# Seven block products instead of eight in 28 projection tiles of a hybrid encoder step

## The chip, the core and the metric

The kernel runs on one core of a Trainium2 chip. The metric is the device time of one execution in microseconds, first instruction to last and what lies around it. The core has five engines that run unsynchronised: TensorE (PE; its weight loads are listed as PEld), VectorE (DVE), ScalarE (ACT), GpSimd (POOL) and SyncE (SP), whose queue issues most DMAs.

## What is computed

One layer for 1088 tokens (1024 of a new stream, 64 of a running one), all in float32:

```
y = x @ w_in                      # (1088 x 1024) @ (1024 x 8720), split by columns into
                                  # qa, ka, va, za | q/k/v of B, a, b, z_B | g_A, g_B
A: rotary on 16 of 64 dims of qa, ka; attention over the own 64-token chunk and 2 before it,
   with a sink per head;          Y_A = (attn * silu(za)) @ w_o_attn
B: causal conv + SiLU, l2norm, gated delta rule in chunks of 64, gated RMSNorm;
                                  Y_B = (rmsnorm(o) * silu(z_B)) @ w_o_delta
x' = LayerNorm(alpha * x + (sig(g_A) * Y_A + sig(g_B) * Y_B) @ w_out)
```

It also returns the last keys and values, the conv tail and the delta states.

## The kernel before

The model dimension lies on the partitions. `w_in` is cut into tiles of 128 output channels. A float32 product is made of three matmuls of a reduced-precision type: each operand is split into a high part (a copy on ACT, L85) and a low part (a subtraction on DVE, L86), and `mm3` adds hi*hi, hi*lo and lo*hi in one PSUM bank. `ring` holds the split x: eight tiles of 128 rows by 1088 tokens, hi and lo.

A projection tile (`project`) runs over three token groups of 384, 384 and 320 columns, each 8 k-tiles by 3 matmuls: 72 matmuls. Each group has a bank of the pool `pj` (three banks; the pool `bg` has five), and `evac` takes it out. `weights` loads a tile of 512 KB and splits it, one tile ahead.

Stages, in order: load and split x; two key tiles (`branch_a_keys`); `vab`, which gives values and the a, b columns with x as the stationary and 272 weight columns as the moving operand; 8 query tiles and 8 z_A tiles, in the first of which `gates` is woven (the decay of branch B, two small matmuls on its results); attention, woven with 13 merge-gate tiles; four head pairs of branch B, woven with their projections, the last 3 gate tiles (`GATES`), z_B and the output product of A; the output product of B; `w_out` and LayerNorm.

`weave(chain, fill)` writes TensorE's order by hand: each step of the chain says how many columns of fill follow it (`UNIT` = 8797 for attention). TensorE's instructions stay in that order. On the other engines and in the DMA queue a scheduler orders by priority; what is under `urgent` goes first. A tile of a pool with `bufs=n` waits until one of n buffers is free. All queues are in order at run time.

An attention unit (36 of them: 9 chunk pairs, 2 key groups, 2 halves) is `scores`, `flip` (6 transposes) and `values`. Before, iteration i runs values of unit i-2, flip of i-1, scores of i. Keys and the z_A gates stay in SBUF, queries come by DMA.

## Time and profile before

| | us |
|---|---|
| median of 3 runs | 1417.84 (1416.69 to 1418.1) |
| the profiled execution | 1418.09 |
| its span, first to last instruction | 1416.3 |
| TensorE busy | 1395.6 |
| DVE, ACT, POOL busy | 914.9, 566.3, 124.9 |
| mean granted TensorE clock | 0.998 |

The profiled execution takes 1.8 us more than its span. Matmuls overlap in the array, so the duration of one is longer than its distance to the next; where TensorE is busy without a break, the pace is the length of the stretch over the number of matmuls.

### The profile page before, as it was taken

To read this page: it belongs to the slowest core of one execution; us is meant where nothing else is said; L and a number is where in the kernel's file an instruction comes from. 1 tells how busy PE (TensorE), PEld (TensorE's weight loads), DVE (VectorE), ACT (ScalarE), POOL (GpSimd) and SP (SyncE) were. 2 spreads that over 40 slices of the span, in tenths; PEclk is the share of its full clock that TensorE was granted. 3 is DMA by queue.
4 is the path that set the end of the run, shared out by engine and by line. 5 is a ranking of instruction groups with operands and counts; after the bars stand their busy time and mean duration, and the time that the engine had idled before them with its cause. 6 is when DMAs were issued, how large, how long until landed. Compare 5 with 4: busy or idle time off the path is not lost.

```text
span 1416.3 us, 29219 instructions
## 1 busy us (share of the span) xinstructions
PE 1395.6 (99%) x11514; PEld 1303.3 (92%) x11514; DVE 914.9 (65%) x2290; ACT 566.3 (40%) x1576; POOL 124.9 (9%) x301
## 2 busy tenths in 40 slices
PE   8999999999999999999999999999999999999997
PEld 8999999899999999988999889988999889999886
DVE  5477522566555457967796777867788554555676
ACT  5333321344444344356633665256534442322000
POOL 0000000000000013121221113021221100000000
PEclk9999999999999999999999999999999999999999
DMA  8123572233432410210321103210435326564221
GB/s 275 44 108 147 204 187 66 89 102 99 144 95 90 142 50 31 72 36 16 89 83 58 31 26 104 81 52 18 156 122 182 97 76 205 170 218 144 95 90 75
DMA packets 81176, 147.52 MB, mean 104 GB/s; under 512 B 10896, under 2 KB 60304, under 8 KB 79760
## 3 DMA queue, kind: packets, MB, share of 16 engines
q1 hardware_dynamic: 67552, 135.17, 29.3%
q10 hardware_dynamic: 13488, 10.49, 2.4%
q8 instruction: 91, 1.49, 0.4%
q14 instruction: 45, 0.37, 0.1%
HBM read 101.39 MB, written 44.24 MB: 103 GB/s over the span
## 4 chain that ended last, share of the span: by engine, by line
PE 89%; DVE 6%; ACT 3%; issue 1%; DMA 1%; SPq 0%; POOL 0%; DVEq 0%; ACTq 0%
PE pj L103 66%; PE bg L103 19%; PE bg L106 4%; DVE acc L586 2%; PE pj L106 1%; ACT whi L85 1%; DVE t2k L689 0%; DVE wlo L86 0%; ACT acc L584 0%; DVE plb L593 0%; DVE t2k L691 0%; DVE ring L86 0%; DMA pl<-xT 0%; DMA plb<-prodB 0%; ACT qs L776 0%
## 5 line engine op out<-in xcount | busy, mean ns | idle before, releaser
L103 PE MATMUL pj<-ring,whi 128*128 128x384 f32 (+1 forms) x3696 | 930.5, 331 | 0.0
L103 PEld LDWEIGHTS pj<-ring,whi 128*128 128x128 f32 x3696 | 648.8, 188 | 9.9 <-issue 8.6
L103 PE MATMUL pj<-ring,wlo 128*128 128x384 f32 (+1 forms) x1848 | 611.1, 331 | 0.0
L103 PEld LDWEIGHTS pj<-ring,wlo 128*128 128x128 f32 x1848 | 347.5, 188 | 5.0 <-issue 4.6
L86 DVE TENSOR_TENSOR wlo<-wraw,whi 128x1024 fp32r<-128x1024 f32 (+2 forms) x86 | 100.9, 1173 | 78.1 <-ACT whi L85 69.3
L586 DVE SCALAR_TENSOR_TENSOR acc<-pre,sm,acc 128x384 f32<-128x384 f32 (+1 forms) x216 | 134.3, 627 | 24.6 <-ACT acc L584 17.8
L85 ACT ACTIVATE whi<-wraw 128x1024 fp32r<-128x1024 f32 (+2 forms) x86 | 87.5, 1018 | 103.9 <-PE pj L103 86.9
L103 PE MATMUL pj<-pl,ring 128*128 128x512 f32 (+2 forms) x432 | 94.5, 337 | 0.0
L482 ACT ACTIVATE P<-bg,nm 128x192 f32<-128x192 f32 (+2 forms) x136 | 54.5, 410 | 57.8 <-DVE nm L475 57.8
L103 PEld LDWEIGHTS pj<-pl,ring 128*128 128x128 f32 x432 | 68.4, 188 | 8.1
L103 PE MATMUL bg<-ring,whi 128*128 128x384 f32 (+1 forms) x240 | 62.0, 342 | 5.1 <-ACT ring L85 5.1
L798 DVE SCALAR_TENSOR_TENSOR S<-S,dec,bg 128x128 f32<-128x128 f32 x128 | 38.7, 344 | 42.4 <-PE bg L103 41.5
L587 ACT ACTIVATE gt<-acc 128x384 f32<-128x384 f32 (+1 forms) x72 | 36.4, 506 | 72.1 <-DVE acc L586 71.8
L776 ACT ACTIVATE qs<-bg,egs 64x128 f32<-64x128 f32 x128 | 46.5, 363 | 29.9 <-DVE R L773 28.4
L593 DVE SCALAR_TENSOR_TENSOR plb<-gt,acc 128x384 f32<-128x384 f32 (+1 forms) x96 | 43.1, 461 | 18.1 <-ACT gt L587 18.0
L773 DVE SCALAR_TENSOR_TENSOR R<-bg,negc,t2k 64x128 f32<-64x128 f32 x128 | 44.6, 348 | 14.7 <-PE bg L103 13.4
L103 PEld LDWEIGHTS bg<-ring,whi 128*128 128x128 f32 x240 | 44.8, 197 | 6.2 <-ACT ring L85 5.6
L584 ACT ACTIVATE acc<-pre,sm 128x384 f32<-128x384 f32 (+1 forms) x72 | 42.8, 597 | 15.4 <-DVE plb L593 6.2
L568 POOL MEMSET pre<- 128x3 f32 x24 | 2.4, 101 | 521.0 <-DMA gB_d<-gt 459.1
L103 PE MATMUL pj<-wolo,ring 128*128 128x512 f32 (+1 forms) x120 | 45.0, 375 | 0.0
L483 DVE TENSOR_TENSOR smm<-smm,es 128x4 f32<-128x4 f32 (+1 forms) x36 | 5.9, 163 | 58.9 <-ACT P L482 58.9
L806 ACT ACTIVATE w1k<-plb 128x128 f32<-128x128 f32 x68 | 21.0, 309 | 56.9 <-DVE plb L804 45.3
(225 smaller groups left out, 1822.8 us busy)
## 6 DMA issues: line engine op xcount, KB each, us to landing
wraw<-w_tiles SPq DMA_DIRECT2D x80, 512.0 KB, 3.7
q_d<-pl SPq DMA_DIRECT2D x4, 2176.0 KB, 7.4
q<-q_d SPq DMA_DIRECT2D x64, 128.0 KB, 2.9
plb<-prodA SPq DMA_DIRECT2D x8, 544.0 KB, 4.6
plb<-prodB SPq DMA_DIRECT2D x8, 544.0 KB, 5.2
pl<-k_d SPq DMA_DIRECT2D x8, 512.0 KB, 7.5
prodA<-pl SPq DMA_DIRECT2D x2, 2048.0 KB, 8.0
t2k<-zs_d ACTq DMA_DIRECT2D x16, 256.0 KB, 3.2
```

Of the source, the lines that this page charges most:

```text
L85: self.nc.scalar.activation(hi, raw, AF.Copy)
L86: self.nc.vector.tensor_tensor(lo, raw, hi.bitcast(F32), ALU.subtract)
L103: self.tc.keep_in_program_order(self.nc.tensor.matmul(o, l, r, start=start, stop=stop))
L106: self.tc.keep_in_program_order(self.nc.tensor.transpose(o, x, self.ident))
L482: nc.scalar.activation(P[:, hf, k], ps[:, k], AF.Exp, bias=nm[:, hf, b : b + 1], scale=0.125, accum_out=sm[:, hf, b : b + 1])
L584: nc.scalar.activation(acc[:, :w], pre[:, 0:w], AF.Copy, scale=cw(0))
L586: nc.vector.scalar_tensor_tensor(acc[:, :w], pre[:, j : j + w], cw(j), acc[:, :w], ALU.mult, ALU.add)
L587: nc.scalar.activation(th[:, :w], acc[:, :w], AF.Tanh, scale=0.5)
L593: nc.vector.scalar_tensor_tensor(o, v(th), 1.0, v(acc), ALU.add, ALU.mult)
L773: nc.vector.scalar_tensor_tensor(R[HS[h]], ks[HS[h], col[h]], self.negc[HS[h], p, c : c + 1], e["vs"][HS[h], i], ALU.mult, ALU.add)
L776: nc.scalar.activation(qs[HS[1 - h]], ks[HS[1 - h], col[h]], AF.Copy, scale=self.egs[HS[1 - h], p, c : c + 1])
L798: nc.vector.scalar_tensor_tensor(Sn[:, h], S[:, h], self.egl[h][:, p, c : c + 1], kv[:, 0:128], ALU.mult, ALU.add)
```

## The change

The gate tile of the last head pair moves to the front (`GATES`), so the front has 32 tiles: 2 of keys, 2 of z_A done as before (`early`), and 28 done in 14 pairs. A pair of tiles is one product of a 2x2 block of weights (two tiles by two halves of the model dimension) with a 2x2 block of x (two halves of the model dimension by two sets of token quarters). `stream` does it with seven block products instead of eight: each is 4 k-tiles by 3 matmuls by 2 quarters of 272 columns. Four sums of weight blocks (`weights7`, per pair) and four of x blocks (`sums_x`, once) are made on GpSimd, then split as before. The seven results are summed in three accumulators A, B, C: A goes on collecting after copies of it have been taken out (`keep`), C likewise, and B is one product. The last two products of a pair (`rest`) run behind the first product of the next one. Wide jobs (7, before attention) do both quarters of a product in turn in two banks each; narrow ones (7, in attention) one quarter after the other.

The fourth x sum takes the place of half of `ring`'s tiles 0 to 3 (`place_last`); `restore_x` loads that half of x again before the head pairs. Queries are laid out so that only the first pair is rotated; keys and queries go to DRAM in pieces and keys come back per unit pair; z_A goes to DRAM and comes back per unit pair. The rotation of keys has one buffer each for `rraw`, `rsh`, `klo`; the two plain tiles' evictions use `rraw` and `rsh`, the scratch of `gates` uses `klo`. In attention, iteration i runs values of unit i-3, flip of i-2, scores of i, and both banks of a flip come from `bg`.

The core of the diff:

```diff
-GATES = (0, 1, 1, 1)
+GATES = (0, 1, 1, 0)
...
+    def sums_x(self):
+        self.T = {}
+        late, parts = [], []
+        sub = lambda d, x, y: self.nc.gpsimd.tensor_tensor(d, x, y, ALU.subtract)
+        for k in range(4):
+            (b11, b12), (b21, b22) = (
+                [x.rearrange("p (g h n) -> p h g n", g=2, h=2)[:, h] for h in range(2)] for x in (self.raw[k], self.raw[4 + k]))
+            t3 = self.t(self.vb, [128, 2, HN], "t3")
+            t4 = self.t(self.vb, [128, 2, HN], "t4", bufs=4)
+            sub(t3, b22, b12)
+            sub(b11, b12, b11)
+            sub(b22, b22, b11)
+            sub(t4, b21, b22)
+            late.append(t4)
+            yield
+            for i, x in ((2, b22), (1, b11), (3, t3)):
+                d = self.T[i, k] = self.t(self.rp2, [128, 2, 2, HN], "ring2", F32R, bufs=12)
+                self.split(d[:, 0], d[:, 1], x, True)
+            yield
+        with self.urgent():
+            self.place_last(late)
...
+    def place_last(self, src):
+        for k in range(4):
+            d = self.ring[k].rearrange("p s (g h n) -> p s h g n", g=2, h=2)[:, :, 1]
+            self.split(d[:, 0], d[:, 1], src[k])
...
+    def restore_x(self):
+        raws = []
+        for j in range(2):
+            raw = self.t(self.wp, [128, 2, 2, HN], "wraw", bufs=2)
+            for k in range(2):
+                src = self.I["xT"][2 * j + k].rearrange("p (g h n) -> p h g n", g=2, h=2)[:, 1]
+                self.nc.sync.dma_start(raw[:, k], src)
+            raws += [raw[:, 0], raw[:, 1]]
+        with self.urgent():
+            self.place_last(raws)
...
+    def weights7(self):
+        nc = self.nc
+        out = []
+        with self.urgent():
+            raw = []
+            for m in range(2):
+                r = self.t(self.wp, [128, KT, 128], "wraw", bufs=2)
+                nc.sync.dma_start(r, self.I["w_tiles"][self.wn + m])
+                raw.append(r)
+            self.wn += 2
+            a11, a12, a21, a22 = (raw[m][:, 4 * k : 4 * k + 4] for m in range(2) for k in range(2))
+            S = self.t(self.ws, [128, 2, 4, 128], "sums")
+            s1, s2, s3, s4 = S[:, 0], S[:, 1], a21, a12
+            sub = lambda d, x, y, op: nc.gpsimd.tensor_tensor(d, x, y, op)
+            sub(s1, a21, a22, ALU.add)
+            sub(s2, s1, a11, ALU.subtract)
+            sub(s3, a11, a21, ALU.subtract)
+            for i, x in enumerate((a11, a12, s2, s1, s3, a22, s4)):
+                if i == 2:
+                    sub(s4, a12, s2, ALU.subtract)
+                pool, tag, bufs = ((self.wp, "whi", 2), (self.wp, "wlo", 2), (self.ws, "wx", 3))[(0, 1, 2, 0, 1, 2, 2)[i]]
+                w = self.t(pool, [128, KT, 128], tag, F32R, bufs=bufs)
+                self.split(w[:, :4], w[:, 4:], x)
+                out.append((w[:, :4], w[:, 4:]))
...
+    def product(self, ps, w, name, g, first, last):
+        hi, lo = w
+        for k in range(4):
+            xh, xl = self.operand(name, k, g)
+            for i, (l, r) in enumerate(((hi, xh), (hi, xl), (lo, xh))):
+                self.mm(ps[:, :HN], l[:, k], r, first and k == 0 and i == 0, last and k == 3 and i == 2, True)
+                yield HN
...
+    def stream(self, jobs):
+        nc = self.nc
+        tail = None
+        def keep(ps):
+            u = self.t(self.ws, [128, HN], "u", bufs=6)
+            with self.urgent():
+                nc.scalar.activation(u, ps[:, :HN], AF.Copy)
+            return u
...
+            W = self.weights7()
+            for gs in ((0, 1),) if wide else ((0,), (1,)):
+                cols = [(2 * g * HN, (2 * g + 1) * HN) for g in gs]
+                bank = lambda: [self.ps() if i else self.pjt() for i in range(len(gs))]
+                def both(banks, w, name, first, last, gs=gs, W=W):
+                    for ps, g in zip(banks, gs):
+                        yield from self.product(ps, W[w], name, g, first, last)
+                A = bank()
+                yield from both(A, 0, "B11", True, False)
+                p1 = [keep(ps) for ps in A]
+                if tail:
+                    yield from tail
+                B = bank()
+                yield from both(B, 1, "B21", True, True)
+                for ps, c, p in zip(B, cols, p1):
+                    evac(0, c[0], ps[:, :HN], p)
+                yield from both(A, 2, "T2", False, False)
+                u2 = [keep(ps) for ps in A]
+                C = bank()
+                yield from both(C, 3, "T1", True, False)
+                yield from both(A, 4, "T3", False, False)
+                u3 = [keep(ps) for ps in A]
+                for ps, c, u in zip(C, cols, u3):
+                    evac(1, c[1], ps[:, :HN], u)
+                def rest(evac=evac, both=both, cols=cols, A=A, C=C, u2=u2):
+                    yield from both(A, 5, "T4", False, True)
+                    for ps, c in zip(A, cols):
+                        evac(1, c[0], ps[:, :HN], None)
+                    yield from both(C, 6, "B22", False, True)
+                    for ps, c, u in zip(C, cols, u2):
+                        evac(0, c[1], ps[:, :HN], u)
+                tail = rest()
+        yield from tail
...
+    def land(self, dst, ps, add):
+        with self.urgent():
+            if add is None:
+                self.nc.scalar.activation(dst, ps, AF.Copy)
+            else:
+                self.nc.vector.tensor_tensor(dst, ps, add, ALU.add)
...
+    def plain(self, abt):
+        nc = self.nc
+        work = self.early()
+        sums = self.sums_x()
+        self.weave(self.gates(abt), work)
+        for _ in sums:
+            for _ in range(18):
+                next(work, None)
...
+    def early(self):
+        nc = self.nc
+        for t in range(2):
+            def ev(g, a, n, ps):
+                th = self.t(self.vb, [128, 384], ("rraw", "rsh")[g % 2], bufs=1)[:, :n]
+                nc.scalar.activation(th, ps, AF.Tanh, scale=0.5)
+                nc.vector.scalar_tensor_tensor(th, th, 1.0, ps, ALU.add, ALU.mult)
+                nc.sync.dma_start(self.zA[t, :, a : a + n], th)
+            yield from self.project(ev, soon=True)
...
+        gb = scr[:, 0:144].rearrange("p (t c) -> p t c", c=8)
         g4 = gb.rearrange("p (t two) c -> p t two c", two=2)
         nc.vector.tensor_copy(g4[0:64, :, 0, :], abt[0:64, :, 0:8])
...
-        self.rqp = rq = self.tc.tile_pool(name="rq", bufs=1)
-        self.rq = rq.__enter__()
...
+        def put(gp, src, dst):
+            n = src.shape[-1]
+            for s, part in enumerate(self.key_parts(src)):
+                for hf in range(2):
+                    nc.sync.dma_start(self.k_d[gp, :, 2 * s + hf, dst : dst + n], part[HS[hf]].bitcast(F32))
...
-                raw, sh = self.rope(ps, a, n)
+                raw, sh = (self.t(self.vb, [128, 384], x, bufs=1)[:, :n] for x in ("rraw", "rsh"))
+                nc.scalar.activation(raw, ps, AF.Copy)
+                self.rope(raw, sh, a, n, KSWAPMASK)
...
-                for o, c in ((a, slice(0, w)), (SEQ + 128, slice(w, n))):
-                    if c.stop > c.start:
-                        nc.vector.tensor_tensor(self.kT[:, gp, o : o + c.stop - c.start], raw[:, c], sh[:, c], ALU.add)
-        nc.sync.dma_start(self.O["o_nkp"], self.kT[:, :, SEQ - 128 : SEQ])
-        nc.sync.dma_start(self.O["o_nks"], self.kT[:, :, KW - 128 : KW])
...
+    def key_parts(self, src):
+        n = src.shape[-1]
+        parts = [self.t(self.vb, [128, 384], x, F32R, bufs=1)[:, :n] for x in ("rsh", "klo")]
+        self.split(*parts, src)
+        return parts
...
+    def load_keys(self, gp, c0, n):
+        k = self.t(self.at, [128, 2, 2, 256], "keys", F32R, bufs=2)
+        for half in HS:
+            src = self.k_d[gp, :, :, c0 : c0 + n]
+            self.nc.sync.dma_start(k[half].rearrange("p s h x -> p (s h) x")[:, :, :n].bitcast(F32), src)
+        return k
...
+                    with self.urgent():
+                        self.split(*parts, ps)
+                else:
+                    raw = self.t(self.rq, [128, HN], "rraw", bufs=4)
...
+                    for s in range(2):
+                        dst = self.qd[s, 128 * j : 128 * j + 128].rearrange("p (c m i) -> p c m i", m=2, i=CH)[:, :, m]
+                        w, c = q[:, s].bitcast(F32), 0 if g == 0 else 32
+                        nc.sync.dma_start(dst[:, 9 * g : 9 * g + 8], w[:, c : c + 512].rearrange("p (c i) -> p c i", i=CH))
+                        nc.sync.dma_start(dst[:, 8, c : c + 32], w[:, 512 - 16 * c : 544 - 16 * c])
+            return ev
...
+        def jobs():
+            yield True, query(0)
+            yield True, gate(self.zA, 2, True)
+            for j in range(1, 4):
+                yield True, query(j)
+            yield True, gate(self.zA, 4, True)
+            yield True, gate(self.zA, 6, True)
+            self.done = True
+            for i in range(0, 16 - sum(GATES), 2):
+                yield False, gate((self.gA, self.gB)[i // 8], i % 8, False)
...
         elif cp == 0:
-            spans = [(0, 128, 0, 64), (1, 64, 0, 128)]
+            spans, window = [(0, 128, 0, 64), (1, 64, 0, 128)], (0, 128)
...
+        if u == 0:
+            self.keys = self.load_keys(gp, *window)
...
+            for r0, base, n in ((0, 0, 16), (16, 128, 48)):
+                base += 2 * n * (2 * gp + u)
+                src = self.qd[s, base : base + 2 * n].rearrange("(h r) x -> r h x", h=2)[:, :, 256 * cp : 256 * cp + 128 * nb]
+                nc.sync.dma_start(dst[r0 : r0 + n], src)
...
         for hf in range(2):
-            ps = self.pjt() if hf else self.ps()
+            ps = self.ps()
...
-            if i > 1:
-                cp, gp, u = unit = units[i - 2]
+        for i in range(len(units) + 3):
+            if i > 2:
+                cp, gp, u = unit = units[i - 3]
...
+            if 1 < i <= len(units) + 1:
+                unit = units[i - 2]
                 PT[unit] = self.flip(unit[0], P.pop(unit))
             if i < len(units):
                 P[units[i]] = self.scores(*units[i])
...
+                        self.consts()
+                        self.branch_a_keys()
+                        self.plain(self.vab())
+                    with scope("gsp") as self.gsp:
+                        with scope("rq") as self.rq:
+                            self.load_rope(self.rq, "ropeq")
+                            work = self.front()
+                        with scope("at") as self.at:
+                            self.weave(self.attention(), work)
+                            self.drain(work)
+                        self.first = self.weights()
+                        self.restore_x()
             with tc.tile_pool(name="mp", bufs=1) as self.mp:
-                with tc.tile_pool(name="pla", bufs=2) as self.pl:
```

## Rows read from the trace of the kernel before

**Rows 1.** The page: busy time of TensorE, its 40 slices, the granted clock.
```profile
PE 1395.6 (99%) x11514; PEld 1303.3 (92%) x11514; DVE 914.9 (65%) x2290; ACT 566.3 (40%) x1576; POOL 124.9 (9%) x301
...
PE   8999999999999999999999999999999999999997
...
PEclk9999999999999999999999999999999999999999
```

**Rows 2.** Busy time by stretch (us; count in brackets): plain tiles; attention.
```profile
72.00:250.00 178.00, 178.00 (x1083) 178.00 (x1082) 91.15 (x177) 48.18 (x85) 0.00 (x0) 1.00 0.44 142
280.00:480.00 200.00, 200.00 (x1616) 181.85 (x1615) 118.15 (x373) 90.03 (x332) 0.00 (x0) 1.00 0.34 112
```

**Rows 3.** Timeline of TensorE, 44 to 60 us: matmuls of 272 columns.
```profile
43.74 13.91 PE L103 MATMUL pj<-pl,ring 128*128 128x272 f32 x109
```

**Rows 4.** Chain that ended last, 300 to 317 us: fill, then one attention unit.
```profile
303.52 4.06 PE pj L103 x27
307.58 0.97 PE bg L103 x16
...
310.22 4.02 PE pj L103 x23
```

**Rows 5.** Timeline of ACT, 331 to 334.3 us: four exponentials, a fill eviction.
```profile
331.22 0.42 ACT L482 ACTIVATE P<-bg,nm 128x192 f32<-128x192 f32 x1 [1.78 <-DVE nm L475]
...
332.82 0.21 ACT L482 ACTIVATION_READ_ACCUMULATOR P<-bg,nm 128x1 f32 x1
333.77 0.49 ACT L441 ACTIVATE gt<-pj 128x384 f32<-128x384 f32 x1 [0.73 <-PE pj L103]
```

**Rows 6.** Groups by shape: busy us, mean ns, then idle before them.
```profile
L85 ACT ACTIVATE whi<-wraw 128x1024 fp32r<-128x1024 f32 x80 | 84.6, 1058 | 102.6 <-PE pj L103 86.9 <-PE bg L103 7.3 <-DMA wraw<-w_tiles 3.6
...
L103 PE MATMUL pj<-pl,ring 128*128 128x272 f32 x192 | 24.4, 289 | 0.0
...
L712 POOL TENSOR_TENSOR U<-V,sm 128x512 f32<-128x512 f32 x16 | 17.0, 1061 | 66.7 <-DVE V L741 66.6
...
L292 ACT ACTIVATE V<-pj 128x256 f32<-128x256 f32 x8 | 3.1, 385 | 17.1 <-PE pj L103 17.1
```

**Rows 7.** Timeline of ACT and DVE, 14 to 16 us: splits of 512 columns.
```profile
14.35 0.62 ACT L85 ACTIVATE whi<-wraw 128x512 fp32r<-128x512 f32 x1
...
15.01 0.69 DVE L86 TENSOR_TENSOR wlo<-wraw,whi 128x512 fp32r<-128x512 f32 x1
```

**Rows 8.** Timeline of DVE, 32 to 69 us: key rotation, then the gates.
```profile
32.41 0.56 DVE L354 TENSOR_TENSOR rsh<-rsh,cs 128x384 f32<-128x384 f32 x1 [4.95 <-DMA cs<-rope]
...
64.39 0.23 DVE L310 COPY gb<-bg 64x72 f32<-64x72 f32 x1
...
68.09 0.22 DVE L324 TENSOR_TENSOR gg<-gg,ea 128x68 f32<-128x68 f32 x1
```

**Rows 9.** DMA issues: count, KB each, median us from issue to landing.
```profile
wraw<-w_tiles SPq DMA_DIRECT2D x80, 512.0 KB, 3.7
...
plb<-prodB SPq DMA_DIRECT2D x8, 544.0 KB, 5.2
...
gA_d<-gt SPq DMA_DIRECT2D x16, 192.0 KB, 1.9
...
o_nkp<-kT SPq DMA_DIRECT2D x1, 128.0 KB, 2.2
```

**Rows 10.** Timeline of SyncE's queue: two issues, how long each holds it.
```profile
334.29 0.33 SPq L442 DMA_DIRECT2D gA_d<-gt  x1
...
336.76 0.58 SPq L463 DMA_DIRECT2D q<-q_d  x1
```

**Rows 11.** Chain that ended last, 1180 to 1240 us: last fill tiles.
```profile
1190.84 14.92 PE pj L103 x93
1205.76 12.00 PE bg L103 x72
```

More of the change, by code (lines that the diff above doesn't have):

```diff
@@ L203, in load_x @@
                 if g > 0:
[L204 to L205 removed]
+                    for k in range(KT):
+                        load(k, a, n, nc.sync)
                 for kt in range(KT):
                     xk = self.ring[kt]
[L208 removed]
+                    self.split(xk[:, 0, a : a + n], xk[:, 1, a : a + n], raw[kt][:, a : a + n])
     def fetch(self, src, raw, order=range(KT)):
@@ L1121, in tables @@
             rope[64 * h + 8 + i, 1] = sin[:, i]
+    ropeq = np.zeros((128, 2, NT), np.float32)
+    for i in range(128):
+        ropeq[i, 0] = cos[:, i % 8]
+        ropeq[i, 1] = sin[:, i % 8] * (1 if i % 16 >= 8 else -1)
     i = np.arange(128)
```

268 lines of the change are left out of this document (141 added, 127 removed).

## The prediction

> **What bounds the kernel now.** I read first the page's busy times and slices: TensorE is busy 99% of the span, in all forty slices, at the full granted clock [rows 1]. Busy is not yet paced, so I then took the stretches [rows 2]: in 178 us of plain tiles 1083 matmuls, 164.4 ns each, a mean over 384, 384 and 320 columns. The distance grows with columns: in `vab`, which has the very shape of the new matmuls, 109 of 272 columns take 13.91 us, of which the last one's own 289 ns is not distance [rows 3, 6]: (13.91 - 0.289) / 108 = 126.1 ns. So TensorE's stream is the path, and time is a sum of paces plus what makes it wait. The chain shows the same in attention: fill of 4.06 us, a unit of 2.64 us, and no other engine between [rows 4]. DVE and ACT are 59% and 45% busy there [rows 2].
>
> **What the change removes.** A plain tile is 72 x 0.1644 = 11.84 us, two are 23.67. A pair by seven products is 7 x 4 x 3 x 2 = 168 matmuls of 272 columns: 168 x 0.1261 = 21.18 us. Fourteen pairs save 14 x 2.49 = 34.8 us. The number of matmuls rises by a sixth and eats part of the eighth saved in columns. The bound: if the records of the `vab` stretch miss some, the pace is lower; 1% lower gives 3 us more, so the cut is 34.8 to 38. The gate tile moved to the front is among the 28. It is missing as fill for the last head pair: behind the last norm stand 14.92 + 12.00 us of fill before the next product [rows 11], 15 after the move, against a store of about 2 us, a load of 5.2 and a split of some 2.5 [rows 9]: hidden, and if not, about 1 us for each us late.
>
> **What it adds on the other engines.** Per pair: ACT seven half splits of 0.62, six copies of 0.39, eight evictions of about 0.39 = 9.8 us, where two tiles had 2 x 1.06 and six evictions of 0.49 = 5 [rows 5 to 7]. DVE: seven halves of 0.69 and six additions of about 0.4 (an estimate, from ACT's 0.39 for the like size) = 7.2, where it had two of about 1.2. In attention 4.1 of each 6.7 us is fill, so ACT goes from 45% to about 60% and DVE from 59% to about 72%. Neither becomes the bound. POOL has four sums of 512 per pair, 1.06 us each by [rows 6], and 16 for x, some 18 us beside keys, values and plain tiles: hidden, since the first of them is wanted two products into the first pair. SP: a unit had two query issues of 0.58, now four, one of keys, one of z_A in or out, two stores and weights: about 4 us of 6.7 [rows 10]. A late store blocks the loads behind it; queries have three buffers, which is 13 us of lead. `weights7` can load only after the last two splits of the pair before, which wait for the delayed tail: 9.1 + 1.4 + 3.7 (landing [rows 9]) + 1.3 (split) = 15.5 of 21.2 us: hidden with 5 to spare. `restore_x` has 1.5 us of the last product and 36 matmuls, 5.9 us, over four splits of 0.7: hidden. For all these together I take 2 us, bounds 0 and 8: any of them comes late in single places.
>
> **Added wait one: the front.** Keys now go through one buffer each. A key group is shuffle, two products, an addition (0.56 each), a split (0.5 and 0.56), then stores that must land (1.9 to 2.2 us, [rows 9]) before `rsh` is free: about 5.1 us a turn. The first can't be rotated before the table lands at 32.4 us [rows 8]; six groups, two extra pieces for the running stream and two for the cache end near 82 us. `gates` takes `klo` as its scratch. From its copies to its result took 64.39 to 68.3 us [rows 8], 4.7 with the copies ahead. TensorE comes to the matmuls on that result at about 68.2 us, 8.7 us into the first plain tile. If the scratch comes last, they start at 87: 18.8 us of standing, for behind them in TensorE's fixed order are the plain tiles and every pair. If it slips into the gap in which the second-last group waits (klo free at about 62 us), they start in time, and then the plain tiles' evictions wait for `rraw`, about 5 us; in the next gap (69 us), 6 us. Bounds 0 and 19. I take 6: two of three orders give it, and a buffer that falls free goes to whoever is ready.
>
> **Added wait two: the hand-offs in attention.** Of a narrow half, three steps reuse a bank one product later: the copy of A before T3, the copy of A before T4, and the eviction of A before the next B. A product is 12 x 0.126 = 1.51 us, with the issue of the last matmul 1.64. The copy can start 0.29 us after that issue [rows 6] and takes 0.39: 0.86 us to spare. ACT is in order. Behind one exponential with its accumulator read (0.6 us) nothing is lost; behind that and a half split (0.62), 0.4 us; behind all four exponentials, which run from 331.22 to 333.03 [rows 5], about 1.05. Where an attention unit falls into the gap (a third of the gaps) nothing is lost. 14 halves x 3 = 42 hand-offs: bounds 0 and 44 us. The nearest row, an eviction of fill that found ACT idle [rows 5], stands near the lower end; with ACT at 60% I take 0.2 us, 8.4 in all. `flip` now holds two `bg` banks, so a unit wants six of five; the sixth is freed by exponentials that end at 333.03, 0.7 us before that fill's eviction [rows 5], and is within the same bounds. Transposes a unit later cost nothing: P has three buffers, and what they wait for has a unit more to come.
>
> **Sum.** 1418.1 - 34.8 + 6 + 8.4 + 2 = 1399.7 us for the profiled execution, 0.25 above the median: 1399.5, said as 1400.
>
> **Rivals.**
> *The whole cut arrives.* ACT always takes the copies first and the gates get their buffer in time: 1418.1 - 34.8 + 0 to 8 = 1383 to 1391. For it: waits on TensorE are now nearly nil and ACT has 40% to spare. Chance 0.25.
> *The front stands its full 18.8 us*: 1383.3 + 18.8 + 10.4 = 1412.5. For it: program order puts all key pieces before the scratch. Against: its first copy is ready long before them. Chance 0.12.
> *The cut is just eaten*, 1415 to 1421: chance 0.05.
> *Slower: ACT serves hand-offs behind its exponentials.* 1383.3 + 6 + 44 + 2 = 1435. It decides from a mean of (34.8 - 8 + 2.8) / 42 = 0.70 us per hand-off. For it: `scores` runs at a better priority than fill, and an exponential that waits for DVE holds what is behind it, 1.78 us in [rows 5]. Against: copies are `urgent`. Chance 0.10.
> *The change doesn't do what it says, since matmuls cost by count.* If the new ones came no faster than the old mean, 168 x 0.1644 = 27.6 us a pair, 55 us more in all: 1473 before any wait; from 141 ns (23.67 / 168) the cut is gone. Against it: 126.1 ns in the same shape [rows 3]. Chance 0.01. The Trainium skill, TensorE: Matmul & The Clock Gate, section Back-to-back issue gap, speaks for it: it puts streams of weight load and matmul at about 81 ns for 128 columns and 131 for 512. By a line between them, an estimate, 272, 320 and 384 columns would cost 99.8, 106 and 114.3 ns, a pair 16.06 us plain and 16.76 by seven: 9.8 us lost over 14 pairs, so some 1428 without any wait. By that rule the trace disagrees: 164.4 and 126.1 ns lie far above it and rise 38.3 ns for 90.7 columns.
>
> **How the numbers follow.** The forecast, some 10 to 27 us off (1391 to 1408), has 0.45, what is left 0.02 beyond the ends. The likeliest sum is 1400. The range 1384 to 1416 leaves out the slow rivals (0.11), half of the eaten cut and the last part of the full cut: 0.18. A measurement here tells 0.2%, 2.8 us, from no change. Faster by that: 0.45 + 0.25 + 0.12 + most of the rest = 0.84; within it 0.05; slower 0.11.
>
> **What would show it.** In the profile after: 168 matmuls of 272 columns per pair at 126 ns, TensorE's matmul count up by 14 x 24 = 336; one standing of TensorE between 65 and 90 us, released by the gates' chain or by an eviction waiting for `rraw`; many short waits of `pj` matmuls on ACT copies between 250 and 480 us, summing to under 15 us; POOL busy from the front on; the head pairs unchanged in length but for one tile. Wrong is the cut if the pace is over 130 ns; the front if TensorE stands for nothing or for over 12 us; the hand-offs if ACT's copies are waited for over 20 us; and all of it if weights or queries are waited for in the DMA queue.

## The result, and the profile after

The kernel got slower: 1450.66 us median (1446.86 to 1451.94) against 1417.97, a ratio of 1.0226 [1.0204, 1.0249]. The forecast was 1400, 1384 to 1416. The profiled execution, the fastest of the four, took 1446.86 us, 47 more than the recorded sum of 1399.7.

The page of the kernel after, its lines that answer to [rows 1]: busy times, TensorE's slices, the granted clock.

```profile
PE 1375.4 (95%) x11850; PEld 1280.2 (89%) x11850; DVE 988.8 (68%) x2404; ACT 626.6 (43%) x1764; POOL 228.8 (16%) x373
...
PE   8839999989999999999999999999998999999997
...
PEclk9969999999999999999999999999999999999999
```

There are 336 more matmuls, as forecast, and TensorE is busy 20 us less. But its third slice (72 to 108 us) fell to 3 tenths. Stretches of the same kernel; the columns are start and end, length, busy us and count of TensorE, of its weight loads, of DVE, ACT and POOL, then the granted clock:

```profile
180.00:260.00 80.00, 80.00 (x641) 80.00 (x640) 42.54 (x81) 35.55 (x81) 19.68 (x15) 1.00 0.69 166
262.70:490.00 227.30, 214.02 (x1859) 195.01 (x1857) 159.34 (x464) 118.77 (x439) 30.30 (x24) 0.98 0.60 165
95.20:99.30 4.10, 4.10 (x17) 4.10 (x18) 1.66 (x4) 1.92 (x3) 1.27 (x1) 0.50 0.00 0
99.60:106.00 6.40, 6.40 (x41) 6.40 (x40) 1.69 (x3) 1.99 (x4) 1.29 (x1) 1.00 0.08 28
```

Pure products run at 80.00 / 641 = 124.8 ns, where [rows 3] gave 126.1: the cut itself is there. In attention (second row) TensorE stands 13 of 227 us, where [rows 2] showed it busy throughout. The last two rows show a cost that no step of the prediction had: after the standing the granted clock is 0.50, the 1.2 GHz level, for the first matmuls, and then 1.00 again. What TensorE waited for, in all and at most:

```profile
PE bg L108 <- DVE klo L495: 28.7, 1, 28.7
PE pj L108 <- DVE gs L407: 5.6, 1, 5.6
...
PE pj L108 <- DVE gt L1124: 4.2, 1, 4.2
PE bg L108 <- ACT PT L719: 3.0, 2, 2.7
PE bg L108 <- DVE z L763: 2.9, 3, 1.4
...
PE pj L108 <- ACT u L359: 2.0, 3, 1.2
```

One wait is most of it: the gates' result `klo`. The copies `u`, the hand-offs on which the prediction spent 8.4 us, are the last line: 2.0 us in the whole kernel, of which 0.3 us lie in attention. To see why the scratch came so late, the timelines of SyncE's queue, VectorE, GpSimd and TensorE in the front, side by side in time (start, length; in brackets the idle time before and what ended it):

```profile
64.36 1.18 SPq L540 DMA_DIRECT2D k_d<-klo  x2
...
74.38 1.18 SPq L540 DMA_DIRECT2D k_d<-klo  x2
...
77.47 1.18 SPq L540 DMA_DIRECT2D k_d<-klo  x2
78.75 0.53 SPq L558 DMA_DIRECT2D rraw<-cache_k  x1
...
85.99 1.10 SPq L540 DMA_DIRECT2D k_d<-klo  x2
```

```profile
70.11 1.08 DVE L91 TENSOR_TENSOR wx<-sums,wx 128x512 fp32r<-128x512 f32 x1 [1.81 <-ACT wx L88]
71.12 0.68 DVE L91 TENSOR_TENSOR wx<-wraw,wx 128x512 fp32r<-128x512 f32 x1
71.72 0.48 DVE L524 TENSOR_TENSOR rsh<-rsh,cs 128x320 f32<-128x320 f32 x1
...
88.49 0.19 DVE L479 COPY klo<-abt 64x72 f32<-64x72 f32 x1 [0.21 <-DMA k_d<-klo]
...
92.51 1.23 DVE L491 SCALAR_TENSOR_TENSOR klo<-klo 128x68 f32<-128x68 f32 x1 [0.32 <-ACT klo L490]
93.78 1.37 DVE L495 TENSOR_TENSOR klo<-klo 128x68 f32<-128x68 f32 x1
```

```profile
92.33 1.33 POOL L271 TENSOR_TENSOR t<-ring,ring 128x544 f32<-128x544 f32 x1 [21.68 <-issue]
93.73 1.33 POOL L271 TENSOR_TENSOR ring<-ring,ring 128x544 f32<-128x544 f32 x1
```

```profile
95.20 0.70 PE L108 MATMUL bg<-klo,u 128*128 128x68 f32 x2 [28.67 <-DVE klo L495]
```

The scratch takes the slot after every key piece has been stored from it, the order of the rival with the full 18.8 us, and it comes later than there: the rotation of the last key group (L524) stood behind two splits of the first weight pair's sums, which VectorE had waited for; a load lies in the sequence; and the chain from 88.49 to 95.15 us is 6.7 us and not 4.7. Its last two pieces end as GpSimd's two x sums end and take 1.23 and 1.37 us; the like piece took 0.22 us in the kernel before [rows 8].

The first product `X,MT` of head pair 0 starts at 598.4 us before and at 632.6 after, 34.2 later; by the recorded sum it would start 6.6 earlier (-34.8 + 11.8 for the moved tile + 16.4). So 41 of the 47 us are lost ahead of it. I place some 37: 22.7 in the standing beyond the 6, 4.1 in gaps for x sums and splits between 115 and 160 us, 2.9 in attention beyond the two terms, and an estimated 7.8 from the clock (the distances of matmuls in the stretches at 0.50, less those of the same shapes elsewhere in this trace). The other 6 are at the last head pair: the wait for `gt` (L1124) and 1.5 of slower matmuls behind it.

### The profile page after: what moved, and what is told of

Same layout as the page of the kernel before. It is cut to its first block, busy times and chain, and to the rows that moved or that the text cites. A ratio compares the mean times of both kernels' runs of the same rounds, so it can differ in the third digit from the quotient of the medians.

```text
span 1445.1 us, 30842 instructions
## 1 busy us (share of the span) xinstructions
PE 1375.4 (95%) x11850; PEld 1280.2 (89%) x11850; DVE 988.8 (68%) x2404; ACT 626.6 (43%) x1764; POOL 228.8 (16%) x373
## 5 line engine op out<-in xcount | busy, mean ns | idle before, releaser
L108 PE MATMUL pj<-ring,whi 128*128 128x384 f32 (+2 forms) x2856 | 678.5, 328 | 4.2 <-DVE gt L1124 4.2
L108 PEld LDWEIGHTS pj<-ring,whi 128*128 128x128 f32 x2856 | 482.4, 190 | 15.0 <-issue 13.7
L108 PE MATMUL pj<-ring,wlo 128*128 128x384 f32 (+2 forms) x1680 | 464.9, 321 | 0.2
L108 PEld LDWEIGHTS pj<-ring,wlo 128*128 128x128 f32 x1680 | 288.9, 189 | 4.9 <-issue 4.0
L108 PE MATMUL pj<-ring,wx 128*128 128x272 f32 x756 | 109.4, 294 | 10.5 <-DVE gs L407 5.6
L108 PEld LDWEIGHTS pj<-ring,wx 128*128 128x128 f32 x756 | 101.3, 193 | 12.1 <-DVE gs L407 5.8
L108 PE MATMUL bg<-ring,whi 128*128 128x384 f32 (+2 forms) x408 | 84.7, 318 | 4.3 <-ACT ring L88 4.3
L108 PE MATMUL pj<-pl,ring 128*128 128x512 f32 (+1 forms) x240 | 70.1, 375 | 0.0
L108 PE MATMUL bg<-ring,wlo 128*128 128x272 f32 (+2 forms) x288 | 63.7, 308 | 0.0
L108 PE MATMUL bg<-keys,q 128*128 128x192 f32 (+2 forms) x272 | 44.2, 289 | 7.3 <-ACT PT L719 3.0
```

What stands on the lines that cost most here:

```text
L108: self.tc.keep_in_program_order(self.nc.tensor.matmul(o, l, r, start=start, stop=stop, skip_group_check=skip))
```

## The experiments

Theory A: the loss lies in the front's shared single slots and what follows from them. Rivals: the supply of x sums on GpSimd, attention (hand-offs, `gs`, banks), the moved gate tile. Times are medians. The ratio, with its 95% interval, is to the kernel before on the same chip, whose medians lie between 1416.94 and 1417.97 us in all of these runs; "less than the change" is against 1450.66 us.

**The scratch in another slot.**

```diff
-        scr = self.t(self.vb, [128, 384], "klo", bufs=1)
+        self.spare = self.t(self.vb, [128, 2 * KT * 272], "wt")
+        scr = self.spare[:, 2304:2688]
```

> The gates' scratch takes the slot of the v/ab weights, which nothing reads after the v/ab tiles (about 62 us), in place of the slot that the key pieces rotate through (free at 88.5 us). Theory A (the front's shared single buffers cost most of the loss): the standing of 28.7 us before the second gates product goes, but the evictions of the two plain tiles still sit behind the cache key pieces in the slots of the key path until about 86 to 88 us, so with three accumulators TensorE stands 10 to 16 us at the fourth group of the plain tiles instead; 1430 to 1440. Rival (the loss lies in the supply of x sums or in attention): everything that is saved here comes back as a wait for the x sums; 1446 to 1452.

1442.15 us, 1.0174 [1.0159, 1.0189]: 8.5 less than the change. TensorE's longest wait in this kernel:

```profile
PE pj L108 <- DVE rraw L463: 14.6, 1, 14.6
```

As theory A said, the standing of 28.7 us is gone and the wait moved to the plain tiles' evictions, which sit in `rraw` behind the same key pieces. The two waits of the prediction were not alternatives: the second stood hidden behind the first.

**The plain tiles' evictions too.**

```diff
-                th = self.t(self.vb, [128, 384], ("rraw", "rsh")[g % 2], bufs=1)[:, :n]
+                th = self.spare[:, 384 * (3 * t + g) :][:, :n]
```

> The same, and the six evictions of the two plain tiles have pieces of their own in the slot of the v/ab weights. Theory A: no standing over 3 us between 60 and 100 us, the granted clock stays up there, and the start of head pair 0 comes 30 to 40 us earlier than in the changed kernel; 1407 to 1420. Rival (the x sums on GpSimd are late by themselves): a wait of 10 us or more for the T operands after 86 us; 1425 to 1440. Rival (attention): little, 1440 or more.

1429.91 us, 1.0092 [1.0075, 1.0109]: 20.8 less than the change, so the shared slots are the largest single part. But it misses its range: 6.3 us for the gates' chain at 67 us and 3.9 for x sums near 101 us remain, each followed by half clock, and attention is untouched.

**The last gate tiles.** The changed kernel with two tiles at the last head pair (`GATES = (0, 1, 1, 2)`), and the kernel before with its last one moved (`(0, 1, 1, 0)`).

> The changed kernel with two gate tiles at the last head pair again, so 12 narrow tiles by products and not 14. The front and attention up to there are the same. Theory (the moved gate tile was cover): the gap of 4.4 us at the first eviction of the attention output goes, and the stretch at half clock after it (3.4 us more), while one pair of plain tiles costs 2.5 us more than seven products; 1443 to 1448. Rival (the moved tile is only moved): 1449 to 1454.

> The kernel before with only the one gate tile moved from the last head pair to the front; everything else is as before. Theory (that tile was cover for the chain of the last pair): TensorE waits 3 to 6 us near the first eviction of the attention output, with a stretch at half clock after it; 1421 to 1427. Rival (it is only moved, as the prediction had it): 1417 to 1419.

The first took 1462.66 us, 1.0323 [1.0307, 1.0338], beyond both expectations. With 12 narrow tiles the fill ends at 505 us and attention's last units run alone, mostly at half clock; this stretch shows it:

```profile
512.00:526.00 14.00, 13.60 (x65) 9.21 (x63) 5.61 (x26) 3.16 (x16) 0.85 (x3) 0.56 0.31 85
```

From its first product of scores to its last of values, attention takes 255.8 us; the changed kernel's 269.0 less one pair's 21.2 would be 247.8. From head pair 0 on the run is 24.0 us longer, the price of two tiles (23.7): the wait for `gt` is gone, but waits of 1.0 to 1.3 us and a stretch at half clock stand there instead, so nothing is won. The last 3.7 us lie ahead of attention, where the edit changes nothing.

The second took 1422.22 us, 1.0038 [1.0023, 1.0053], with this wait, which the kernel before doesn't have:

```profile
PE pj L103 <- DVE gt L908: 3.4, 1, 3.4
```

So moving that one tile costs some 5 us by itself, 3.4 of them in this wait: "hidden" was wrong. The evictions of the first attention-output tile stand on VectorE behind the last pair's chain, as these lines of the changed kernel show, and the tile had been the fill beside that chain:

```profile
1115.00 0.73 DVE L905 TENSOR_TENSOR t2k<-t2k,t2k 128x338 f32<-128x338 f32 x1
1115.65 1.41 DVE L1124 SCALAR_TENSOR_TENSOR gt<-gt,pj 128x384 f32<-128x384 f32 x3
```

**Single waits, each on the version with both slots (1429.91).** Four runs: the x sum pieces `t3`, one each and not one for four; the order `GATES = (0, 1, 0, 1)`; the stores of gate tiles on ScalarE's queue; the transposes one unit behind the scores and the values two, as in the kernel before. The fence shows the core of the first, third and fourth edit.

```diff
-            t3 = self.t(self.vb, [128, 2, HN], "t3")
+            t3 = self.spare[:, 2688 + 544 * (k - 1) :][:, :544].rearrange("p (g n) -> p g n", g=2) if k else self.t(self.vb, [128, 2, HN], "t3")
...
-                nc.sync.dma_start(dst[t + m, :, a : a + HN], th)
+                nc.scalar.dma_start(dst[t + m, :, a : a + HN], th)
...
-            if 1 < i <= len(units) + 1:
-                unit = units[i - 2]
+            if 0 < i <= len(units):
+                unit = units[i - 1]
```

The x sum pieces:

> On the version whose gates' scratch and plain-tile evictions have places of their own (1429.9): each x sum b22 - b12 has a piece of its own too, in place of one piece for all four, so GpSimd no longer waits from one k to the next for a split. Theory (that one piece is what makes the T operands late): the gaps of 3.2 and 1.3 us near 100 us and the half clock after them (6.9 us long) go, some 6 to 9 us; 1421 to 1425. Rival (the pinned splits on ScalarE are what is late): 1428 to 1431.

The order of gate tiles:

> On the same version (1429.9), the last gate tile stands with the last head pair again, and one fewer with the pair ahead of it, so 14 narrow tiles stay in products. Theory (the tile at the last pair is cover for its chain): the gap of 4.2 us near 1093 us and the stretch at half clock after it go; 1421 to 1426. Rival (the gap moves to the pair ahead, whose chain loses the tile): 1428 to 1432.

The stores:

> On the same version (1429.9), the stores of the gate tiles by products are issued on ScalarE's queue in place of SyncE's. Theory (at 268 us these stores sit on SyncE behind a store that waits for the attention values and six query loads, so the five gs pieces come free late): the gap of 6.0 us there goes, with the stretch at half clock after it, 6 to 10 us in all; 1420 to 1424. Rival (ScalarE pays for the issues, and its other hand-offs come later): 1428 to 1436.

The transposes:

> On the same version (1429.9), the transposes of P come one unit after their scores, and the values two, as in the kernel before. As the prediction had it, a unit more or less between them is hidden: 1428 to 1432. Rival (with the products' hand-offs ahead of them on VectorE and ScalarE the transposes need the second unit): the waits of TensorE for P grow by over 10 us; 1438 to 1470. Rival (two units hold a bank or a buffer longer and cost the gaps of 1 to 2 us at 306, 380 and 417 us): 1422 to 1427.

| edit | median, us | ratio |
|---|---|---|
| x sum pieces | 1426.63 | 1.0066 [1.0051, 1.0081] |
| order of gate tiles | 1429.81 | 1.0094 [1.0069, 1.0120] |
| stores on ScalarE's queue | 1426.12 | 1.0060 [1.0045, 1.0075] |
| transposes one unit behind | 1432.03 | 1.0111 [1.0079, 1.0143] |

The first lost its gaps for x sums near 100 us, but the wait for the gates' chain beside GpSimd's now denser work grew from 6.3 to 11.0 us. The second moved part of the gap to the pair ahead, the rival's case. The fourth is no difference: the transposes a unit later cost nothing, and bring nothing here. The third removed the gap of 5.7 us, yet, like the first, gained less than its theory. In the version without it (both slots, 1429.91) the cause can be read, first on SyncE's queue, then on ScalarE:

```profile
267.30 0.38 SPq L765 DMA_DIRECT2D prodA<-z  x1
267.73 2.91 SPq L677 DMA_DIRECT2D q<-q_d  x6
270.69 1.90 SPq L623 DMA_DIRECT2D zA_d<-gs  x4
```

```profile
272.83 0.43 ACT L620 ACTIVATE gs<-gs 128x272 f32<-128x272 f32 x1 [1.88 <-DMA zA_d<-gs]
```

Four stores of finished gate pieces wait behind a store of attention values (its data end at 267.28 us on VectorE) and six query loads; ScalarE then has no free `gs`, VectorE waits for ScalarE, and TensorE for VectorE.

**The gates' product later, and all together.** The first run has the gates' second product behind the plain tiles, with 48 and 18 in place of the 24 and 12 shown; the second has this with 24 and 12, and `t3` and the stores as well.

```diff
-        yield 24 * 384
+        yield 96 * 384
         ps = self.ps()
...
+            for i, n in enumerate(early):
+                if i >= 24 and (i - 24) % 12 == 0:
+                    next(sums, None)
+                yield n
```

Two more runs each add one edit to the second: the weight sums on VectorE, or the first tile of the attention output in three `bg` banks.

```diff
-            sub = lambda d, x, y, op: nc.gpsimd.tensor_tensor(d, x, y, op)
+            sub = lambda d, x, y, op: nc.vector.tensor_tensor(d, x, y, op)
```

```diff
-                pss[g] = self.ps() if bool(w) == EDGE else self.pjt()
+                pss[g] = self.ps() if bg or bool(w) == EDGE else self.pjt()
...
-            yield from self.project(ev, edge=t in (0, 7), w=None if t else w)
+            yield from self.project(ev, edge=t in (0, 7), w=None if t else w, bg=t == 0)
```

The gates' product later:

> On the version whose gates' scratch and plain-tile evictions have places of their own (1429.9): the gates' second product comes behind the two plain tiles and not behind their first group, so its chain on VectorE and ScalarE has some 20 us of cover and not 4. Theory (what is left of the standing at 66.6 us is this chain behind key work and weight splits): the gap of 6.4 us goes, with the 6.8 us at half clock after it, 6 to 10 us; 1420 to 1424. Rival (the wait for the x sums at 99 us grows by what is won here, since they hang on the same two engines): 1427 to 1431.

All together:

> All of these together: places of their own for the gates' scratch, the plain tiles' evictions and the four x sums, the gates' second product behind the plain tiles, the steps of the x sums from the second plain group on, and the gate stores on ScalarE's queue. If the standings are independent, their gains add up from 1429.9: 6 to 10 (gates), 4 to 9 (x sums), 4 to 8 (gs); 1405 to 1414, below the kernel before. Rival (one queue behind all of them, so the wait moves on each time): 1418 to 1424.

With the weight sums on VectorE:

> The joint version, with the four sums of each weight pair on VectorE in place of GpSimd. Theory (GpSimd's sums stretch VectorE's multiplies of P from 1.0 to 3 to 4 us, and the score banks come free late): the gaps of 1 to 3 us at 293, 343, 378, 418 and 434 us shrink to under 3 us in sum, 4 to 8 us less than the joint version. Rival (VectorE, 69% busy, pays 2.6 us for each pair, and its hand-offs come later): the same as the joint version or up to 5 us more.

With three `bg` banks:

> The joint version, with the first tile of the attention output accumulated in three banks of the other pool, so the next tile's three banks are free while its evictions wait on VectorE. Theory (only this eviction, behind the chain of the last pair on VectorE, makes TensorE wait at 1091 us): that gap of 4 us and the half clock after it go; 4 to 7 us less than the joint version. Rival (the chain of the last pair needs those banks): 0 to 5 us more.

| version | median, us | ratio |
|---|---|---|
| gates' product later | 1429.58 | 1.0077 [1.0053, 1.0101] |
| all together | 1425.12 | 1.0050 [1.0033, 1.0068] |
| and weight sums on VectorE | 1431.20 | 1.0087 [1.0066, 1.0108] |
| or three `bg` banks | 1421.91 | 1.0039 [1.0022, 1.0056] |

The gains did not add up, and in the first three the rivals came nearer than the theories, if not within their ranges each time. In the first, 5.1 us came back as a wait for the copies `u` at 92 us. With the banks the wait of 4.0 us for `gt` became one of 3.1 us for the z_B tile's eviction; from head pair 0 on the profiled execution takes 811.6 us, against 812.3 without them, so most of the 3.2 us lies where this edit does not work. The weight sums on VectorE gave its multiplies of P (the scaling of the attention weights by their row sums) back their 315 ns, but the queue is in order, and the sums wait at its head for a weight load, 13.8 us in attention:

```profile
L330 DVE TENSOR_TENSOR sums<-wraw 128x512 f32<-128x512 f32 x5 | 3.5, 693 | 13.8 <-DMA wraw<-w_tiles 13.8
```

**What is left: four runs on the last joint version (1421.91).** The first has the first weight pair's sums and splits not ahead of the rest. The other three add one edit each to it: the weight sums cut to 4 of 128 columns, which leaves out most of them, so that the outputs are not the layer's; the multiplies of P on GpSimd; the x sums of k = 1 and 2 from free slots.

```diff
+        with nullcontext() if first else self.urgent():
             self.wn += 2
```

```diff
-            s1, s2, s3, s4 = S[:, 0], S[:, 1], a21, a12
-            sub = lambda d, x, y, op: nc.gpsimd.tensor_tensor(d, x, y, op)
+            s1, s2, s3, s4 = a21, a22, a21, a12
+            sub = lambda d, x, y, op: nc.gpsimd.tensor_tensor(d[:, :, :4], x[:, :, :4], y[:, :, :4], op)
```

```diff
-                nc.vector.tensor_scalar(P[:, hf, k], P[:, hf, k], sm[:, hf, b : b + 1], None, ALU.mult)
+                nc.gpsimd.tensor_scalar(P[:, hf, k], P[:, hf, k], sm[:, hf, b : b + 1], None, ALU.mult)
```

```diff
+            if k == 1:
+                pair = self.t(self.rp2, [128, NT], "ring2", bufs=12)
+            t3 = pair[:, 544 * (k - 1) : 544 * k].rearrange("p (g n) -> p g n", g=2) if k in (1, 2) else self.t(self.vb, [128, 2, HN], "t3")
```

The first weight pair:

> On the last joint version (first tile of the attention output in the other pool's banks; 1421.9): the sums and splits of the first weight pair no longer stand ahead of the plain tiles' evictions. Theory (in the front ScalarE waits 5.6 us for GpSimd's weight sums at 71 us with the plain tiles' tanh behind it): the gap of 4.8 us at 75 us goes, the plain tiles end earlier; 1415 to 1419. Rival (the products' first operands are then late and the gap of 5.6 us at 87 us grows): 1421 to 1426.

Short weight sums:

> The same as the run above, with each of the four sums of a weight pair cut to 4 of its 128 columns, in place; the seven products work with wrong weights, everything else stays. Theory (in attention GpSimd's sums stretch VectorE's multiplies of P): the gaps of 1 to 2.3 us at 338, 375, 412 and 428 us go, 6 to 9 us less than the run above. Rival (the hand-offs and banks of the products themselves): 0 to 3 us less.

P on GpSimd:

> The same as the first of these, with the multiplies of P on GpSimd and not on VectorE. Theory (those multiplies on VectorE are where the time goes): the gaps in attention shrink to under 5 us in sum, 3 to 7 us less than the first. Rival (GpSimd is slower at them and P comes late even two units behind, or its work stretches VectorE's other pieces): 5 to 40 us more.

x sums early:

> The same as the first of these, with the x sums of k = 1 and 2 from free slots of the T operands, so GpSimd can make three of the four before the v/ab tiles end. Theory (GpSimd's x sums from 59 to 73 us stretch VectorE's pieces there from 0.5 to 1.4 us and hold up its weight sums): no standing over 2 us from 60 to 100 us, 4 to 9 us less than the first. Rival (they then stretch the key work on VectorE and the keys come later): 0 to 6 us more.

| version | median, us | ratio |
|---|---|---|
| first weight pair | 1421.14 | 1.0031 [1.0017, 1.0045] |
| short weight sums | 1405.43 | 0.9915 [0.9900, 0.9930] |
| P on GpSimd | 1412.01 | 0.9963 [0.9952, 0.9974] |
| x sums early | 1426.90 | 1.0062 [1.0042, 1.0083] |

The first makes no difference that can be told: its gap at 75 us went, but one of 4.1 us came at 63 us, and the one at 87 us grew from 5.4 to 8.2. The last was slower, as its rival had it; but the gap at 87 us is of the joint edits' own making (below). The second and third are the key to attention. Groups by shape, the multiplies of P: in the kernel before, after, in the first of these four, and in the one with short sums (busy us, mean ns):

```profile
L488 DVE TENSOR_SCALAR P<-P,smm 128x192 f32<-128x192 f32 x120 | 30.5, 316 | 1.1
```

```profile
L701 DVE TENSOR_SCALAR P<-P,smm 128x192 f32<-128x192 f32 x120 | 39.9, 384 | 1.0
```

```profile
L708 DVE TENSOR_SCALAR P<-P,smm 128x192 f32<-128x192 f32 x120 | 40.8, 391 | 1.0
```

```profile
L707 DVE TENSOR_SCALAR P<-P,smm 128x192 f32<-128x192 f32 x120 | 31.6, 315 | 1.0
```

The mean hides that a few carry all of it. One place in the changed kernel, on VectorE, GpSimd and ScalarE:

```profile
396.95 4.14 DVE L701 TENSOR_SCALAR P<-P,smm 128x192 f32<-128x192 f32 x4
401.01 0.43 DVE L407 TENSOR_TENSOR gs<-pj,u 128x272 f32<-128x272 f32 x1
```

```profile
396.95 1.30 POOL L330 TENSOR_TENSOR sums<-wraw 128x512 f32<-128x512 f32 x1 [20.72 <-DVE smm L697]
398.33 1.41 POOL L330 TENSOR_TENSOR sums<-sums,wraw 128x512 f32<-128x512 f32 x1
399.69 1.28 POOL L330 TENSOR_TENSOR wraw<-wraw,wraw 128x512 f32<-128x512 f32 x1
```

```profile
401.47 0.43 ACT L619 ACTIVATE gs<-gs 128x272 f32<-128x272 f32 x1 [3.90 <-DVE gs L407]
401.81 0.46 ACT L719 COPY PT<-bg 128x384 f32<-128x384 f32 x1
```

Four multiplies of 0.3 us take 4.14 us, as long as GpSimd's three sums; behind them wait `gs` on VectorE, behind that the tanh on ScalarE, and behind that the copy that frees a bank: TensorE stands 2.7 us. The Trainium skill, SBUF — State Buffer, section Who interferes with whom, says that VectorE's `tensor_scalar` can use the port pair that it shares with GpSimd, that whoever comes first holds it for its whole instruction, and that the other is fully blocked. The trace agrees: 4.14 us beside the sums, and 315 ns each with short sums.

On GpSimd itself the multiplies take 807 ns, yet the kernel is 9.1 us faster than the first of the four, and short sums give 15.7. Between 262 and 480 us TensorE's waits fell from 6.4 us to 2.3 and 0.8, and more matmuls fit into the stretch (the first of the four, P on GpSimd, short sums):

```profile
262.00:480.00 218.00, 210.52 (x1857) 191.20 (x1858) 157.68 (x448) 118.22 (x427) 30.22 (x24) 0.99 0.61 165
```

```profile
262.00:480.00 218.00, 214.98 (x1925) 195.76 (x1924) 130.23 (x337) 122.14 (x440) 126.79 (x149) 1.00 0.62 168
```

```profile
262.00:480.00 218.00, 216.17 (x1934) 196.93 (x1934) 148.76 (x458) 121.62 (x437) 4.76 (x21) 1.00 0.60 165
```

From its first product of scores to its last of values, attention takes 262.8, 253.9 and 253.2 us in these three: 8.9 and 9.6 us less. So the two edits agree on what the multiplies cost there; the other 5.7 us that short sums save lie ahead of attention. That GpSimd's multiplies can be slow because the transposes come two units later is likely, but no run has both edits.

**Two runs on the front.** The trace of the run with P on GpSimd shows that the joint versions had made a gap of their own on TensorE, from 87 us on:

```profile
93.30 0.64 PE L108 MATMUL pj<-ring,whi 128*128 128x320 f32 x1 [6.11 <-DVE ring L91]
```

```diff
-                if i >= 24 and (i - 24) % 12 == 0:
+                if 24 <= i < 120 and (i - 24) % 12 == 0:
                     next(sums, None)
...
-                self.split(w[:, :4], w[:, 4:], x)
+                self.split(w[:, :4], w[:, 4:], x, first and i > 1)
```

The second hunk is in the second run alone.

The first:

> The joint version with the multiplies of P on GpSimd (1412.0), and the step that puts the T4 sums in the place of x behind the plain tiles. In the joint versions so far it came one group early: the last group of the second plain tile waited for the sums and was computed from them, and not from x, for all but its first matmul. Theory (the gap of 6.1 us at 87 us is this edit's own, with some of the 6.9 us at half clock after it): 1402 to 1408. Rival (the products' first operands are late anyway, and the wait moves to them): 1409 to 1413.

The second:

> The same, with the splits of the first weight pair's sums and last blocks kept behind the plain tiles' evictions on ScalarE's queue. Theory (ScalarE waits 5.6 us for GpSimd's weight sums at 71 us with the plain tiles' tanh behind it): the gap of 4.8 us at 75 us and the half clock after it go, 4 to 8 us less than the run above. Rival (the third product's operand is late then, or VectorE beside GpSimd is what is slow): within 2 us of the run above.

1405.98 us, 0.9922 [0.9908, 0.9935], and 1408.42 us, 0.9940 [0.9927, 0.9952]. The first is within its range, and the fastest that does the whole computation: 11 us below the kernel before, 44.7 below the changed one, 6 above the forecast. Its largest waits but for one of 4.4 us ahead of the first matmul, which the kernel before has too (4.8), and its attention (columns as above):

```profile
PE pj L108 <- DVE wt L469: 4.5, 1, 4.5
...
PE pj L108 <- ACT u L360: 3.9, 6, 0.9
PE bg L108 <- DVE gt L830: 3.6, 1, 3.6
```

```profile
250.00:480.00 230.00, 226.12 (x2015) 205.40 (x2014) 136.21 (x354) 126.41 (x454) 129.94 (x152) 1.00 0.61 165
```

The second run lost the wait at 74 us as said, but one of 4.1 us at 62.8 us came, and it did not pay. The profile names no releaser for it. The matmul behind it reads `abt`, which VectorE finished at 66.82 us, 0.1 us before, behind the rotation of the last key group. That rotation met GpSimd's x sums here; in the run with P on GpSimd it came just ahead of them (first this run, then that one):

```profile
60.36 1.64 DVE L531 TENSOR_TENSOR rsh<-rsh,cs 128x320 f32<-128x320 f32 x1
62.03 1.52 DVE L557 TENSOR_TENSOR rraw<-rraw,rsh 128x320 f32<-128x320 f32 x1
```

```profile
58.79 0.48 DVE L531 TENSOR_TENSOR rsh<-rsh,cs 128x320 f32<-128x320 f32 x1
59.30 0.49 DVE L557 TENSOR_TENSOR rraw<-rraw,rsh 128x320 f32<-128x320 f32 x1
```

The same standing of 4.1 us, with the same slow pieces, is in the profiles of "all together" and of the first weight pair, and not in that of the fastest version. Ahead of the rotation VectorE waits for a key store to land, 3.80 us in this run and 2.30 in that with P on GpSimd; by this reading some 1.5 us there decide whether the front stands.

## Why the prediction was wrong

**The step that failed is added wait one, "Bounds 0 and 19. I take 6".** It measured 28.7 us. "two of three orders give it, and a buffer that falls free goes to whoever is ready" was a guess about the order; what stands in the trace is the program's order, which the text had named as what speaks for the 18.8. The bound of 19 failed too, for it held the other work fixed: the splits of the first weight pair came between the key pieces on VectorE, and the chain was stretched. And the prediction took the evictions' wait for `rraw`, 5 us, as the alternative to the scratch's; it is another 14.6 us behind it. Both slots undone give 20.8 us. The 6.3 us that then still stand before the gates' product are not the prediction's 6: they are the chain's own length behind key work and weight splits, which it did not price.

**POOL's sums, "hidden, since the first of them is wanted two products into the first pair", failed next.** Some 18 us of work on an idle engine were priced by whether it is ready in time. It costs through VectorE: the multiplies of P in attention (8.9 us less with them on GpSimd, 9.6 with short sums), and in the front pieces of 0.2 us that take 1.2 to 1.4, and of 0.5 that take 1.5 to 1.6. The x sums were late as well, by the one `t3`. The sums took 1.28 to 1.41 us, not 1.06.

**Every term took a standing at its length.** In the changed kernel TensorE came back at granted clock 0.50 after the standings of 28.7 and 5.6 us, and the clock fell to it 0.3 and 0.9 us after those of 4.2 and 2.7 us had ended; the stretches at 0.50 cost an estimated 9 us in all. The trace of before could not show it: between TensorE's first matmul and its last, none of its waits reaches 1 us.

**The moved gate tile, "hidden, and if not, about 1 us for each us late", failed** at another place than the one looked at. The text followed the last norm's store; the fill was missed by VectorE's chain at the start of the last pair, 5 us.

**Added wait two was the wrong mechanism.** The copies of the 42 hand-offs cost 0.3 us in attention and not 8.4 (between 240 and 515 us at most 3.1 in any other run), so the rival at 1435 by hand-offs did not occur although the time lies beyond it. Attention lost 11.5 us to three other waits: a store in SyncE's queue behind other waits ("A late store blocks the loads behind it" had it the other way round), the stretched multiplies, and banks held by `z` and `PT`. By the prediction's own terms the copy's slack was 0.96 us (1.64 - 0.29 - 0.39) and not 0.86, which changes nothing here.

**Right were** the cut (124.8 against 126.1 ns, 336 matmuls more), DVE in attention (70%, forecast 72%; ACT, at 52%, stayed under its 60%), and the transposes a unit later at no cost. With the failed steps mended, but for the moved tile, the change gives 1406.

**Open:** what each edit in the front is worth by itself. The joint version and all its kin but the last two runs have a gap at 87 us of that edit's own, and some of their profiled executions have the 4.1 us at 63 us and others not, so the runs on the first weight pair and on early x sums settle nothing there. Some 4 of the 41 us ahead of head pair 0 are not placed, and how much of the last version's remaining waits could go was not tried.

## What to carry to other kernels

When a change makes buffers shared, write down who holds each slot in program order and take that order as the forecast; two waits on one resource are a sequence, and not a choice. An idle engine is not free: ask what its work does to the engine beside it, and which in-order queue it heads. And where TensorE has hardly waited before, price the clock beside the wait: here most of the long standings cost more than their length.

## What was not expected of the hardware

The clock: after the standings of 28.7, 5.6 and 4.2 us in the changed kernel some 4 us of matmuls ran at 0.50, but after the one of 3.4 us in the kernel before with the moved tile none did (granted clock 1.00 from 1091.6 to 1096 us). Like waits can go either way: of the three near 340, 377 and 417 us in attention, 1.8, 2.9 and 1.8 us long, each was followed by a stretch at 0.50 in the profile of "all together"; in that of the version with three `bg` banks (1.4, 2.2 and 2.0 us) none was, and attention took 268.4 us there and 263.3 here. GpSimd's sums hold up VectorE's `tensor_scalar` one for one, 4.14 us for 1.3 us of work. The version with three `bg` banks also spread more, 1419.25 to 1430.6 us over ten runs, where the kernel before spread from 1416.43 to 1419.32 over nineteen.
